# Neighbourhood attention in a transformer block on one core: transposes in 64-row pairs, division after the values, pool outputs as operands at once, first output tiles among the last units

## The chip, the cores and the metric

The kernel runs on one core of a Trainium2 chip. The metric is the device time of one execution in microseconds; three runs of the kernel before gave a median of 1085.58 us (1084.1 to 1085.93). Engines are named as in the profile: PE multiplies matrices and transposes, PEld is its weight load, ACT and DVE work elementwise (ACT: copies, exponentials, squares; DVE: sums, products, minima), POOL does small jobs, SP issues most DMAs. Matrix products accumulate in PSUM, in banks of 128 x 512 float32; everything else lies in SBUF.

## What is computed

One layer of a diffusion transformer block for 1024 latent tokens (a grid of 16 rows by 64 columns) and 256 context tokens, width 1024, all in float32:

```python
h_x = _modulate(x, g_pre_mix, sh1, sc1)              # RMSNorm, scale and shift
h_c = _modulate(ctx, g_pre_mix, csh1, csc1)
u_x, q_x, k_x, v_x = _project(h_x, w_in)             # 8 heads of 64
u_c, q_c, k_c, v_c = _project(h_c, w_in)
s_loc = where(col_mask, q_r @ k_window * scale + bias(rpb), -inf)   # 8 rows x 16 columns
s_ctx = q_r @ k_c * scale                                           # all context keys
p = softmax(concat(s_loc, s_ctx))
attn_x = p_loc @ v_window + p_ctx @ v_c
d = windowed_mean(u_x) - u_x                         # windows 2, 4, 8, 16 by channel group
mix_x = concat(d @ pool_w * pool_scale, attn_x) @ w_out
x = x + gt1 * _rmsnorm(mix_x, g_post_mix)
y_x = square(relu(_modulate(x, g_pre_mlp, sh2, sc2) @ w1)) @ w2
x = x + gt2 * _rmsnorm(y_x, g_post_mlp)
```

## The kernel before

Large products are done in a split form: each float32 operand is written as a rounded high part (a cast, on ACT) and the remainder (a subtraction, on DVE), and `three` (lines 167 to 170) adds high x high, high x low and low x high. Smaller products, among them the scores and values of the attention, are plain float32.

Stages in order of time: the inputs are normalised and transposed; `k`, `v`, `u` and `q` are projected (to about 237 us); the attention runs in units (237 to 368); the output projection `w_out` runs in two halves of 512 columns with 8 token tiles each (`out_group`, from 368); then the MLP, which uses some two thirds of the time.

**Buffers.** `act` holds 33 pages of 128 x 1024 (`page`), `wraw` 4 raw weight tiles (`load`, tag `raw`), `whl` 8 tiles of high or low weights. A new tile of a pool waits until the one whose place it takes has been read for the last time. PSUM has 8 banks: in the attention `ps_s` holds the scores (two tiles of two banks), `ps_t` transposed probabilities (3 banks), `ps_o` the output (1 bank).

**The pool mixer.** For each of 4 groups `pooled` makes the differences `dT` on DVE; `pool_out` multiplies them by `pool_w` on PE and ACT writes the scaled result back into the page `u` (`yT`). These products stand between the `u` and `q` projections, one group late. Later, in eight of the attention's steps (`SPLITS`), `pool_split` splits half a page each into the `mix` operands of the output projection. `background` carries the sums over `w_mod` for the later gates: each step is one weight load and one DVE addition into a page (`acca`, `accb`), and `mod_gate` closes a sum with matrix products (`pga`, `pgb`) on PE.

**A unit** is one pair of heads `j` and one strip of 8 grid columns `m`: 32 units, 128 queries each, all 16 rows of the strip. `scores` computes for both heads (64 rows of the array each) 384 local and 256 context scores (256 and 256 for the two edge strips), and DVE adds the bias table and takes the minimum (scores are negated). `exps` takes exponentials with their sums on ACT. `shares` multiplies the probabilities by the reciprocal sums on DVE. `turn` transposes the probabilities in blocks of 128 x 128 on PE (5 per head, 4 at the edges), `turn_kept` copies them from PSUM on ACT. `values` multiplies them with `v` into `po`, which collects four units; then ACT and DVE split it into `mix` (lines 738 and 739).

**The order** of PE, ACT, DVE and SP in the attention is as written (`in_order`, line 754). The loop's step `i` issues the scores of unit `i`, the transposes of unit `i - 2`, the exponentials of unit `i`, the division of unit `i - 1` and the values of unit `i - 3`; it has three more steps than there are units. The raw output weights are loaded in step 20 and split from step 32 on.

**The output projection**, lines 806 to 819: a tile is 24 matrix products of 512 columns (8 blocks in `order`, three each) into a bank of its own; ACT takes its mean square, and after it DVE multiplies it by the gate `G1` into `mp1`.

Of the kernel before, what the change touches and what calls it, by code (L numbers as in the profile page):

```python
# [79 lines left out]
def hybrid_block(ctx, tc, x, ctx_in, w_mod, b_mod, gp1, gp2, w_in, pool_w, rpb, w_out, w1, w2, vectors,  # L80
# [136 lines left out]
    with tc.tile_pool(name="ps1", bufs=8, space=PSUM) as ps1, tc.tile_pool(name="tmp1", bufs=3) as tmp:  # L217
# [310 lines left out]
        yT, dT = [], []  # L528

        def pooled(g):  # L530
            up, w = yT[g], WINDOWS[g]
# [30 lines left out]
        def pool_out(g, dp):  # L562
            dv = dp.rearrange("p (r m c) -> p m r c", r=QR, m=NM)
            for b in range(2):
                ps = bank(f"py{g}_{b}")
                nc.tensor.matmul(ps, pwt[:, g, :], dv[:, 4 * b : 4 * b + 4], start=True, stop=True)
                nc.scalar.activation(yT[g][:, b * 512 : (b + 1) * 512], ps, AF.Identity, scale=pscol[:, g : g + 1])

        for g in range(4):
# [6 lines left out]
            yT.append(up)  # L576
            dT.append(pooled(g))
            if g:
                pool_out(g - 1, dT[g - 1])
# [41 lines left out]

        for j in range(4):
            queries(j, 0, bank(f"pq{j}_0"), 3 if j > 1 else 0)
            if j == 2:
                pool_out(3, dT[3])
        for j in range(2):
            if j == 0:
                mask_page()
                tables(0)
            queries(j, 1, bank(f"pq{j}_1"), 5 - 5 * j)  # L630


    mix = [[None] * 8 for _ in range(2)]
    with (
        tc.tile_pool(name="ps_s", bufs=2, space=PSUM) as ps_s,
        tc.tile_pool(name="ps_t", bufs=3, space=PSUM) as ps_t,
# [7 lines left out]
        probs, least, sums, turns, turned, outs = {}, {}, {}, {}, {}, {}  # L644
# [42 lines left out]
        def shares(i):  # L687
            ri = sm(f"ri_{i}", 2, 4)
            nc.vector.reciprocal(ri, sums[i])
            for e in range(2):  # L690
                nc.vector.tensor_scalar_mul(probs[i, e], probs[i, e], ri[:, e : e + 1])  # L691

        def turn(i, e):
            j, m = units[i]
            if e < 2:
                if e == 0:
                    turns[i] = [page(f"pt{i}").rearrange("p (e i t) -> p e i t", e=2, i=4), None]
                t = bank(f"T{i}_{e}")
                for c in range(4):
                    nc.tensor.transpose(t[:, c * P : (c + 1) * P], probs[i, e][:, c * P : (c + 1) * P], ident)  # L700
                turned[e] = t
            elif 0 < m < NM - 1:
                t = bank(f"T{i}_x")
                for e in range(2):
                    nc.tensor.transpose(t[:, e * P : (e + 1) * P], probs[i, e][:, 4 * P : 5 * P], ident)
                turned[2] = t

        def turn_kept(i, e):
            if e < 2:
                nc.scalar.copy(turns[i][0][:, e], turned.pop(e).rearrange("p (i t) -> p i t", i=4))  # L710
            elif 2 in turned:
                px = page(f"px{i}")[:, : 2 * P].rearrange("p (e t) -> p e t", e=2)
                nc.scalar.copy(px, turned.pop(2)[:, : 2 * P].rearrange("p (e t) -> p e t", e=2))
                turns[i][1] = px

        def values(i):
            j, m = units[i]
            b = m // 4
            if m % 4 == 0:
                outs[j, b] = ps_o.tile([P, 512], F32, tag="po", name=f"po{j}_{b}")  # L720
            po = outs[j, b]
# [6 lines left out]
            pt, px = turns[i]  # L728
            for c, v in enumerate(vs):
                for e in range(2):  # L730
                    f = (2 * j + e) * HD
                    nc.tensor.matmul(po[e * HD : (e + 1) * HD, (m % 4) * P : (m % 4 + 1) * P], v[:, f : f + HD],  # L732
                                     pt[:, e, c] if c < 4 else px[:, e], start=(c == 0), stop=(c == len(vs) - 1))
            if m % 4 == 3:
                mp = page(f"mix{b}_{4 + j}", F32R)
                hi, lo = (mp[:, o : o + 512].rearrange("p (m t) -> p m t", t=P) for o in (0, 512))
                pv = po.rearrange("p (m t) -> p m t", t=P)[:, :, ::-1]
                nc.scalar.copy(hi, pv)
                nc.vector.tensor_tensor(lo, pv, hi.bitcast(F32), sub)
                mix[b][4 + j] = mp  # L740
# [7 lines left out]
        def pool_split(n):  # L748
            b, g = n // 4, n % 4
            mp = page(f"mix{b}_{g}", F32R)  # L750
            split(yT[g][:, b * 512 : (b + 1) * 512], mp[:, :512], mp[:, 512:])
            mix[b][g] = mp

        with in_order(ET.PE, ET.Activation, ET.DVE, ET.SP):
            for i in range(N + 3):
                if i < N and units[i][1] == 2 and units[i][0] < 3:
                    tables(units[i][0] + 1)
                if i < N:
                    scores(i)
                if 1 < i <= N + 1:  # L760
                    for e in range(3):
                        turn(i - 2, e)
                    for e in range(2):
                        turn_kept(i - 2, e)
                if i < N:
                    exps(i, 0)
                if 1 < i <= N + 1:
                    turn_kept(i - 2, 2)
                full = i > 2 and units[i - 3][1] % 4 == 3
                if i < N and not full:  # L770
                    exps(i, 1)
                if i < 2:
                    queries(2 + i, 1, bank(f"pq{2 + i}_1"), 3 if i == 0 else 99)
                if 0 < i <= N:
                    shares(i - 1)
                if i > 2:
                    values(i - 3)
                if i < N and full:
                    exps(i, 1)
                if i in SPLITS:  # L780
                    pool_split(SPLITS.index(i))
                if i == 20:
                    for kk in kks:
                        raw_o[0, kk] = load(f"wo0_{kk}", pair(w_out, kk, 0, 512))
                if i >= N:
                    wo[kks[i - N]] = high_low(f"wo0_{kks[i - N]}", raw_o[0, kks[i - N]])

    with tc.tile_pool(name="ps2", bufs=8, space=PSUM) as ps2:
# [4 lines left out]
      with ExitStack() as tmp2:  # L793
        tmp = tmp2.enter_context(tc.tile_pool(name="tmp2", bufs=4))

        wo[kks[3]] = high_low(f"wo0_{kks[3]}", raw_o[0, kks[3]])
        for kk in kks:
            raw_o[1, kk] = load(f"wo1_{kk}", pair(w_out, kk, 512, 512))
        G1 = gate_page("a")


        order = (4, 5, 6, 0, 1, 2, 3, 7)
        ssm = [sm(f"ssm{h}", NT) for h in range(2)]
        mp1 = [page(f"mp1_{t}") for t in range(NT)]

        def out_group(h):
            w = wo if h == 0 else {kk: high_low(f"wo1_{kk}", raw_o[1, kk]) for kk in kks}
            hs = slice(h * 512, (h + 1) * 512)
            for t in range(NT):
                b, i = t // 4, t % 4  # L810
                ps = bank(f"pw{h}_{t}")
                for n, k in enumerate(order):
                    mp = mix[b][k]
                    three(ps, mp[:, i * P : (i + 1) * P], mp[:, 512 + i * P : 512 + (i + 1) * P],
                          wk(w, k, 0, 0, 512), wk(w, k, 1, 0, 512), n == 0, n == 7)
                jk = tmp.tile([P, 512], F32, tag="t", name=f"jo{h}_{t}")
                mean_square(jk, ps, ssm[h][:, t : t + 1])
                nc.vector.tensor_tensor(mp1[t][:, hs], ps, G1[:, hs], mul)  # L818
                yield t

        for _ in out_group(0):
# [61 lines left out]
        for t in out_group(1):  # L883
# [411 lines left out]
```

## Time and profile before

| what | value |
|---|---|
| median of three runs | 1085.58 us |
| the profiled execution | 1083.97 us, span of its instructions 1082.2 us |
| granted PE clock, mean | 0.997 of full speed |
| attention, first scores to first output product | 237.69 to 368.66 us |
| output projection, first half | 368.66 us on, 8 tiles |
| MLP, first product | 459.35 us |

A row of the profile's groups gives line, engine, operation, tile written <- tiles read, array rows*columns, shape and count, then busy time, mean duration of one, and idle time before it with what ended it. A row of the timeline starts with the start and the length. The chain of waits is followed back from the last instruction, each piece with its start and length. A matmul's duration contains a fixed time after its columns have streamed, so matmuls that follow each other overlap in it.

### The profile page before, as it was taken

To read this page: it belongs to the slowest core of one execution; us is meant where nothing else is said; L and a number is where in the kernel's file an instruction comes from. 1 tells how busy PE (TensorE), PEld (TensorE's weight loads), DVE (VectorE), ACT (ScalarE), POOL (GpSimd) and SP (SyncE) were. 2 spreads that over 40 slices of the span, in tenths; PEclk is the share of its full clock that TensorE was granted. 3 is DMA by queue.
4 is the path that set the end of the run, shared out by engine and by line. 5 is a ranking of instruction groups with operands and counts; after the bars stand their busy time and mean duration, and the time that the engine had idled before them with its cause. 6 is when DMAs were issued, how large, how long until landed. Compare 5 with 4: busy or idle time off the path is not lost.

```text
span 1082.2 us, 14471 instructions
## 1 busy us (share of the span) xinstructions
PE 1064.0 (98%) x5505; PEld 866.8 (80%) x5505; DVE 684.8 (63%) x1036; ACT 519.3 (48%) x877; POOL 63.4 (6%) x109
## 2 busy tenths in 40 slices
PE   7999999999999999999999999999999999999997
PEld 6788887777777788887888888888888888888885
DVE  5546624555887515599986776665576657556576
ACT  6553021316888613677555545554454334334341
POOL 2020000051220001210000000000000000000001
PEclk9999999999999999999999999999999999999999
DMA  9906740250020307454764444535597775546556
GB/s 342 312 20 207 248 149 0 98 169 2 20 98 1 98 1 220 130 185 140 239 212 149 163 148 132 189 107 180 198 375 252 258 264 178 211 156 213 175 179 210
DMA packets 94265, 179.32 MB, mean 166 GB/s; under 512 B 6898, under 2 KB 39154, under 8 KB 94196
## 3 DMA queue, kind: packets, MB, share of 16 engines
q1 hardware_dynamic: 76644, 144.80, 40.5%
q10 hardware_dynamic: 16272, 29.40, 7.3%
q0 software_dynamic: 1280, 4.21, 1.1%
q8 instruction: 43, 0.70, 0.3%
q14 instruction: 26, 0.21, 0.1%
HBM read 140.62 MB, written 37.76 MB: 165 GB/s over the span
## 4 chain that ended last, share of the span: by engine, by line
PE 91%; ACT 3%; DVE 3%; issue 1%; DMA 1%; POOL 1%; SPq 0%; POOLq 0%; DVEq 0%; ACTq 0%
PE pk L374 4%; PE S L662 4%; PE po L732 3%; PE T L700 3%; PE pyv L168 3%; PE pyz L169 3%; PE pyz L168 3%; PE pyx L169 3%; PE phv L170 3%; PE phz L170 3%; PE pyv L169 3%; PE pyx L170 3%; PE phv L168 3%; PE phz L168 3%; PE phv L169 3%; PE phz L169 3%
## 5 line engine op out<-in xcount | busy, mean ns | idle before, releaser
L945 ACT ACTIVATE c<-c 128x512 f32<-128x512 f32 x48 | 30.4, 634 | 59.7 <-DVE c L1044 23.8
L676 DVE CUSTOM_DVE_ANT_0 sp<-S,tab 128x640 f32<-128x640 f32 (+1 forms) x56 | 42.8, 801 | 21.1 <-PE S L662 21.1
L685 ACT ACTIVATE sp<-sp,nm 128x640 f32<-128x640 f32 (+1 forms) x64 | 52.0, 813 | 7.0 <-DVE nm L676 6.9
L144 DVE TENSOR_TENSOR wpS<-S,wpS 128x512 fp32r<-128x512 f32 x64 | 43.8, 690 | 12.7 <-ACT wpS L143 12.7
L168 PE MATMUL phx<-thB,wpA 128*128 128x512 f32 x128 | 50.0, 391 | 0.9 <-ACT s L1003 0.9
L170 PE MATMUL phx<-thB,wpA 128*128 128x512 f32 x128 | 49.9, 390 | 0.0
L169 PE MATMUL phx<-tlB,wpA 128*128 128x512 f32 x128 | 49.8, 389 | 0.0
L143 ACT CAST wpS<-S 128x512 fp32r<-128x512 f32 x64 | 39.1, 616 | 17.7 <-PE phy L170 7.5
L710 ACT COPY pt<-T 128x512 f32<-128x512 f32 x64 | 34.4, 591 | 15.7 <-PE T L700 13.5
L139 POOL TENSOR_TENSOR ry<-vy,nhalf 128x1 f32<-128x1 f32 x8 | 4.4, 550 | 601.9 <-DVE vy L137 601.9
L700 PEld LDWEIGHTS T<-ident,sp 128*128 128x128 f32 x256 | 27.4, 141 | 10.8 <-ACT sp L685 4.6
L700 PE MATMUL T<-ident,sp 128*128 128x128 f32 x256 | 34.9, 279 | 0.4 <-DVE sp L691 0.4
L946 ACT ACTIVATE c<-c 128x512 f32<-128x512 f32 x48 | 30.4, 632 | 9.7 <-DVE sa L1016 8.9
L818 DVE TENSOR_TENSOR mp<-pw,Ga 128x512 f32<-128x512 f32 x16 | 11.0, 689 | 36.6 <-ACT jo L130 36.6
L691 DVE TENSOR_SCALAR sp<-sp,ri 128x640 f32<-128x640 f32 (+1 forms) x64 | 32.2, 545 | 1.1
L604 POOL TENSOR_TENSOR tab<-msk,U 128x128 f32<-128x128 f32 x48 | 28.1, 620 | 63.1 <-DMA U<-in_rpb 63.1
L1052 DVE TENSOR_TENSOR c<-phz,u 128x512 f32<-128x512 f32 x16 | 11.1, 692 | 32.1 <-PE phz L170 32.1
L130 ACT ACTIVATE jo<-pw 128x512 f32<-128x512 f32 x16 | 9.6, 598 | 40.9 <-PE pw L170 40.9
L168 PEld LDWEIGHTS phx<-thB,wpA 128*128 128x128 f32 x128 | 24.0, 188 | 6.2 <-ACT s L1003 1.3
L662 PE MATMUL S<-kT,q 64*128 64x384 f32 (+1 forms) x128 | 28.9, 495 | 0.0
L170 PEld LDWEIGHTS phx<-thB,wpA 128*128 128x128 f32 x128 | 24.0, 188 | 5.2 <-DVE wpA L144 0.2
L169 PEld LDWEIGHTS phx<-tlB,wpA 128*128 128x128 f32 x128 | 24.0, 188 | 5.0
(881 smaller groups left out, 3262.0 us busy)
## 6 DMA issues: line engine op xcount, KB each, us to landing
b<-in_w SPq DMA_DIRECT2D x64, 512.0 KB, 4.5
hrS<-hdS SPq DMA_DIRECT2D x32, 512.0 KB, 5.5
hrA<-hdA SPq DMA_DIRECT2D x24, 512.0 KB, 5.2
wm<-in_w_mod SPq DMA_DIRECT2D x16, 512.0 KB, 9.7
wa_0w<-in_w SPq DMA_DIRECT2D x16, 512.0 KB, 5.6
wa_1w<-in_w SPq DMA_DIRECT2D x16, 512.0 KB, 4.1
hdA<-c ACTq DMA_DIRECT2D x32, 256.0 KB, 2.1
hdS<-sa ACTq DMA_DIRECT2D x32, 256.0 KB, 4.3
```

The costliest lines, as they stand in the source:

```text
L143: nc.scalar.copy(hi, src)
L144: nc.vector.tensor_tensor(lo, src, hi.bitcast(F32), sub)
L168: nc.tensor.matmul(ps, ahi, bhi, start=first, stop=False, skip_group_check=more)
L169: nc.tensor.matmul(ps, ahi, blo, start=False, stop=False, skip_group_check=more)
L170: nc.tensor.matmul(ps, alo, bhi, start=False, stop=last, skip_group_check=more)
L374: nc.tensor.matmul(pks[b][j], wk(wgt, k, low, j * P, P), r, start=(k == 0 and n == 0), stop=(k == KT - 1 and n == 2))
L662: nc.tensor.matmul(S[e][:, c0 : c0 + keys.shape[1]], q[hs, cols], keys[hs], start=True, stop=True)
L676: nc.vector.tensor_tensor_reduce(out=to, in0=s, in1=bt, scale=1.0, scalar=BIG, op0=add, op1=ALU.min, accum_out=nm)
L685: nc.scalar.activation(sp, sp, AF.Exp, bias=least[i, e], scale=-1.0, accum_out=sums[i][:, e : e + 1])
L700: nc.tensor.transpose(t[:, c * P : (c + 1) * P], probs[i, e][:, c * P : (c + 1) * P], ident)
L710: nc.scalar.copy(turns[i][0][:, e], turned.pop(e).rearrange("p (i t) -> p i t", i=4))
L732: nc.tensor.matmul(po[e * HD : (e + 1) * HD, (m % 4) * P : (m % 4 + 1) * P], v[:, f : f + HD], pt[:, e, c] if c < 4 else px[:, e], start=( ...
```

## The change

The unit's transposes become pairs: the upper and the lower 64 query rows of a block of probabilities are transposed separately, each into a PSUM bank of its own, so that `T` has one bank per row half that holds all eight blocks of both heads. The probabilities are no longer divided. Instead `share` spreads the reciprocal sums over 64 columns per head, and one more pair of transposes turns them. This and the fifth blocks go into the free columns of the values' PSUM tile (`sides` of `pa`), and one ACT copy, `fifth_kept`, brings them to SBUF. `weighed` multiplies the values by the turned reciprocals, one step after the values. Of the two `T` banks ACT copies one and DVE the other.

`pool_out` writes the high part on ACT and the low part on DVE straight from PSUM into `mix`; half of these tiles take the four places of `wraw`. All four groups stand after the first query product of the second half. The background sums end with the queries 3 of the first half. The output weights go to pages, are loaded in steps 9, 14, 20 and 24 and split in halves in eight steps; low parts are made one step after high parts. Output tile 0 is computed in steps 32 to 34, tile 1 after them, both in the two halves of one score tile `po`; the rest follow in `out_group` as before.

```diff
-            if g:
-                pool_out(g - 1, dT[g - 1])
...
+                mp = page(f"mix1_{g}", F32R) if b else wraw.tile([P, 1024], F32R, tag="raw", name=f"mix0_{g}")
+                nc.scalar.activation(mp[:, :512], ps, AF.Identity, scale=pscol[:, g : g + 1])
+                nc.vector.scalar_tensor_tensor(mp[:, 512:], ps, pscol[:, g : g + 1], mp[:, :512].bitcast(F32), mul, sub)
...
+        for j in range(4):
+            queries(j, 0, bank(f"pq{j}_0"), (1, 2, 3, 99)[j])
+        mask_page()
+        tables(0)
+        queries(0, 1, bank("pq0_1"), 0)
+        for g in range(4):
+            pool_out(g)
+        queries(1, 1, bank("pq1_1"), 0)
...
-        tc.tile_pool(name="ps_t", bufs=3, space=PSUM) as ps_t,
+        tc.tile_pool(name="ps_t", bufs=2, space=PSUM) as ps_t,
...
+        pa = ps_o.tile([P, 1024], F32, tag="pa", name="pa")
+        sides = pa.rearrange("p (h f) -> p h f", h=2)[:, :, 256:448]
...
-            for e in range(2):
-                nc.vector.tensor_scalar_mul(probs[i, e], probs[i, e], ri[:, e : e + 1])
+            shares[i] = att.tile([P, P], F32, tag="ri", name=f"rb{i}", bufs=2)
+            nc.vector.tensor_copy(shares[i].rearrange("p (e t) -> p e t", e=2),
+                                  ri.rearrange("p (e o) -> p e o", o=1).to_broadcast([P, 2, HD]))
...
+            def both(to, src):
+                for h, hs in enumerate(halves):
+                    nc.tensor.transpose(to(h), src(hs), ident[hs, hs])
+            both(lambda h: sides[:, h, :HD], lambda hs: shares[i][hs])
+            for e in range(2 if inner else 0):
+                both(lambda h: sides[:, h, (e + 1) * HD : (e + 2) * HD], lambda hs: probs[i, e][hs, 4 * P : 5 * P])
+            for c in range(4):
                 for e in range(2):
+                    o = (4 * e + c) * HD
+                    both(lambda h: t[h][:, o : o + HD], lambda hs: probs[i, e][hs, c * P : (c + 1) * P])
+        def fifth_kept(i):
+            n = (3 if 0 < units[i][1] < NM - 1 else 1) * HD
+            fifths[i] = att.tile([P, 384], F32, tag="px", name=f"px{i}", bufs=4).rearrange("p (h t) -> p h t", h=2)
+            nc.scalar.copy(fifths[i][:, :, :n], sides[:, :, :n])
...
+        def weighed(i):
+            j, m = units[i]
+            if m % 4 == 0:
+                mixed[j, m // 4] = page(f"f{j}_{m // 4}")[:, :512]
+            to = mixed[j, m // 4].rearrange("p (m h t) -> p m h t", h=2, t=HD)[:, m % 4, ::-1, ::-1]
+            nc.vector.tensor_tensor(to, pa[:, (i % 2) * P : (i % 2 + 1) * P].rearrange("p (h t) -> p h t", h=2),
+                                    fifths[i][:, :, :HD], mul)
...
-        SPLITS = (7, 8, 15, 16, 23, 24, 31, 32)
+        LOADS, HALVES = (9, 14, 20, 24), (13, 17, 19, 21, 25, 27, 29, 30)
...
+            for i in range(N + 4):
...
+                if i > 3:
+                    weighed(i - 4)
+                low()
+                if i > 8 and i % 8 == 7:
+                    mixed_split(i // 8 - 1, 1)
+                if i > 0 and i % 8 == 0:
+                    mixed_split(i // 8 - 1, 0)
+                if i in HALVES:
+                    weight_split(HALVES.index(i))
                 if i < N:
                     scores(i)
                 if 1 < i <= N + 1:
+                    turn(i - 2)
+                    fifth_kept(i - 2)
                 if i < N:
                     exps(i, 0)
                 if 1 < i <= N + 1:
+                    turn_kept(i - 2, 0, nc.scalar.copy)
+                if i < N:
+                    exps(i, 1)
+                if 1 < i <= N + 1:
+                    turn_kept(i - 2, 1, nc.vector.tensor_copy)
...
                 if 0 < i <= N:
+                    share(i - 1)
+                if 2 < i <= N + 2:
                     values(i - 3)
+                if i == N:
+                    po = ps_s.tile([P, 1024], F32, tag="S", name="po")
                 if i >= N:
+                    out_sums(po[:, :512], wo, 0, ((0, 1), (2, 3, 4), (5, 6, 7), ())[i - N])
+            out_kept(0, 0, po[:, :512], page("jo0_0")[:, :512])
+            mixed_split(3, 1)
+            low()
+            out_sums(po[:, 512:], wo, 1, range(8))
+            out_kept(0, 1, po[:, 512:], page("jo0_1")[:, :512])
...
-        for _ in out_group(0):
+        for _ in out_group(0, range(2, NT)):
             pass
```

More of the change, by code (lines that the diff above doesn't have):

```diff
@@ L685, in exps, with share @@
             nc.scalar.activation(sp, sp, AF.Exp, bias=least[i, e], scale=-1.0, accum_out=sums[i][:, e : e + 1])
-        def shares(i):
-            ri = sm(f"ri_{i}", 2, 4)
+        def share(i):
+            ri = sm(f"ri_{i}", 2, 2)
             nc.vector.reciprocal(ri, sums[i])
-            for e in range(2):
[L691 to L703, printed above, removed]
-                for e in range(2):
-                    nc.tensor.transpose(t[:, e * P : (e + 1) * P], probs[i, e][:, 4 * P : 5 * P], ident)
-                turned[2] = t
@@ new lines, in turn @@
+        def turn(i):
+            inner = 0 < units[i][1] < NM - 1
+            t = [bank(f"T{i}_{h}") for h in range(2)]
+            turned[i] = t
+            halves = [slice(h * HD, (h + 1) * HD) for h in range(2)]
+            def both(to, src):
[5 more added lines that the diff above has]
+            for c in range(4):
+                for e in range(2):
+                    o = (4 * e + c) * HD
+                    both(lambda h: t[h][:, o : o + HD], lambda hs: probs[i, e][hs, c * P : (c + 1) * P])
@@ L731, in values @@
                     f = (2 * j + e) * HD
[L732 to L740, printed above, removed]
+                    nc.tensor.matmul(pa[e * HD : (e + 1) * HD, cols], v[:, f : f + HD],
+                                     turns[i][:, e, c] if c < 4 else fifths[i][:, :, (e + 1) * HD : (e + 2) * HD],
+                                     start=(c == 0), stop=(c == len(vs) - 1))
@@ new lines, in weight_load, with out_sums @@
+        def weight_load(h, kk):
+            raw_o[h, kk] = page(f"wor{h}_{kk}")
+            nc.sync.dma_start(raw_o[h, kk].rearrange("p (a f) -> p a f", a=2), pair(w_out, kk, h * 512, 512))
+        order = (4, 5, 6, 0, 1, 2, 3, 7)
+        ssm = [sm(f"ssm{h}", NT) for h in range(2)]
+        mp1 = {}
+        def out_sums(ps, w, t, ns):
+            b, i = t // 4, t % 4
+            for n in ns:
+                k, mp = order[n], mix[b][order[n]]
+                three(ps, mp[:, i * P : (i + 1) * P], mp[:, 512 + i * P : 512 + (i + 1) * P],
+                      wk(w, k, 0, 0, 512), wk(w, k, 1, 0, 512), n == 0, n == 7)
```

120 lines of the change are left out of this document (48 added, 72 removed).

## The prediction

> **What bounds the kernel now.** I read the page first, then the chain of waits in order of time, then single stretches.
>
> ```profile
> span 1082.2 us, 14471 instructions
> PE 1064.0 (98%) x5505; PEld 866.8 (80%) x5505; DVE 684.8 (63%) x1036; ACT 519.3 (48%) x877; POOL 63.4 (6%) x109
> ```
>
> PE is busy nearly throughout, so a gain must be PE work removed or one of its few gaps closed. The busy times of the stretches that the diff touches (the units, their tail, the first output half), columns stretch, then PE, PEld, DVE, ACT and POOL:
>
> ```profile
> 253.00:358.00 105.00, 105.00 (x1040) 79.64 (x1037) 82.88 (x216) 89.42 (x208) 12.25 (x24) 1.00 0.10 31
> 358.00:368.00 10.00, 8.55 (x106) 7.25 (x104) 7.71 (x16) 9.63 (x20) 0.00 (x0) 1.00 0.06 13
> 368.00:418.00 50.00, 49.34 (x218) 40.87 (x219) 13.15 (x16) 10.99 (x22) 0.00 (x0) 1.00 0.27 82
> ```
>
> Through the units PE has no idle time, at a granted clock of 1.00, with ACT at 85% and DVE at 79%. The chain gives the pace and the ends:
>
> ```profile
> 234.48 0.38 issue
> ...
> 236.86 0.70 DVE accb L199
> 237.69 1.14 PE S L662 x8
> ...
> 253.78 1.98 PE S L662 x7
> ...
> 357.11 1.06 PE S L662 x8
> ...
> 367.92 0.69 DVE mix L739
> 368.66 0.50 PE pw L168
> ```
>
> Unit 3 starts at 253.78 and unit 31 at 357.11: 28 steps in 103.3 us, 3.69 each. One inner step on PE (first fence) and on its weight loads (second):
>
> ```profile
> 266.23 0.60 PE L662 MATMUL S<-kcT,q 64*128 64x256 f32 x4
> 266.76 1.09 PE L700 MATMUL T<-ident,sp 128*128 128x128 f32 x8
> 267.69 0.38 PE L705 MATMUL T_x<-ident,sp 128*128 128x128 f32 x2
> ```
>
> ```profile
> 265.48 0.30 PEld L662 LDWEIGHTS S<-kT,q 64*128 64x128 f32 x4 [0.17 <-DVE sp L691]
> 266.75 0.86 PEld L700 LDWEIGHTS T<-ident,sp 128*128 128x128 f32 x8 [0.33 <-ACT sp L685]
> 268.00 0.63 PEld L732 LDWEIGHTS po<-pt,v 128*64 128x64 f32 x12 [0.17 <-issue]
> 269.24 0.30 PEld L662 LDWEIGHTS S<-kcT,q 64*128 64x128 f32 x4 [0.17 <-DVE sp L691]
> ```
>
> Scores take 265.48 to 266.75 (1.27), transposes to 268.00 (1.25), values to 269.24 (1.24): 3.76 in all.
>
> **The turn (64-row pairs).** An inner unit had 10 full transposes, an edge unit 8; now 11 and 9 pairs, each two 64-row transposes that move 64 columns, one pair of them for the reciprocal sums. The single durations:
>
> ```profile
> L662 PEld LDWEIGHTS S<-kT,q x128: 182/186/187, 238.0 to 357.6; 64*128 64x128 f32 x128
> ...
> L662 PE MATMUL S<-kT,q x128: 376/482/587, 238.2 to 357.8; 64*128 64x384 f32 x96, 64*128 64x256 f32 x32
> ```
>
> ```profile
> L700 PEld LDWEIGHTS T<-ident,sp x256: 137/141/146, 252.7 to 364.3; 128*128 128x128 f32 x128
> L700 PE MATMUL T<-ident,sp x256: 272/273/332, 252.7 to 364.4; 128*128 128x128 f32 x128
> ```
>
> A full transpose starts every 0.11 us: the two T_x lie in 0.38, and 0.38 - 0.273 = 0.11. The scores are already 64-row pairs: four 256-column matmuls of 0.376 lie in 0.60, so the last pair starts 0.60 - 0.376 = 0.22 after the first: two at once, at 0.22 per 256 columns. A 64-column pair is then 0.055. Its weights: four score loads of 0.187 lie in 0.30, so two run together and the next two start 0.11 later; a transpose's load is 0.046 shorter, which leaves 0.06 for a pair of loads. So a pair costs 0.06 if loads and matmuls overlap as in the scores, 0.11 if something keeps the old rate, and 0.22 if nothing overlaps. I take 0.06, as the scores are the nearest row: same row halves, two banks. The turn falls from 1.10 to 0.66.
>
> Between scores and transposes the loads now idle 0.33. Between one score pair and the next there is no such stretch on PE (0.22 per pair is streaming alone), and the new turn has the scores' 64x128 shape; so I count none, with 0.15 per step (4 us over 28) as the bound if it stays. The Trainium skill (TensorEngine Tiling, Key Properties) says that a change of the tiling mode drains the engine. By that rule the stretch goes, as counted; the three idle stretches of the weight loads, all at a change of shape, agree with it.
>
> **What then ends the step.** The values do not wait for the turn alone. In the changed program's own order every unit's first values matmul waits for ACT's copy of the side strip (the reciprocals and fifth blocks) of the next unit, because both lie in one tile `pa`. The rows for ACT and DVE, columns line, operation, count, busy, mean:
>
> ```profile
> L685 ACT ACTIVATE sp<-sp,nm 128x640 f32<-128x640 f32 x46 | 38.7, 842 | 0.5 <-DVE nm L676 0.5
> L710 ACT COPY pt<-T 128x512 f32<-128x512 f32 x58 | 31.2, 589 | 15.6 <-PE T L700 13.5 <-issue 1.4
> ...
> L713 ACT COPY px<-T_x 128x256 f32<-128x256 f32 x22 | 8.1, 369 | 0.0
> ```
>
> ```profile
> L676 DVE CUSTOM_DVE_ANT_0 sp<-S,tab 128x640 f32<-128x640 f32 x46 | 36.0, 821 | 15.7 <-PE S L662 15.6
> L691 DVE TENSOR_SCALAR sp<-sp,ri 128x640 f32<-128x640 f32 x46 | 23.4, 551 | 0.8
> ...
> L739 DVE TENSOR_TENSOR mix<-po,mix 128x512 fp32r<-128x512 f32 x7 | 4.8, 692 | 4.3 <-ACT mix L738 4.3
> ...
> L689 DVE RECIPROCAL ri<-su 128x2 f32<-128x2 f32 x29 | 4.6, 160 | 0.0
> ```
>
> The strip of 384 columns lies between 0.369 (256) and 0.589 (512): 0.48. From the first strip matmul: two more pairs 0.12, the last one's own time 0.22 (0.273 less 0.055), hand-over 0.04, copy 0.48, hand-over 0.06 (368.60, the end of the mix subtraction, to 368.66): 0.92. The main pairs end within 0.66 plus the 0.17 drain and hide under it. Then values 1.24 and scores up to their last streamed column, 1.19 (266.23 + 0.22 + 0.22 - 265.48): 3.35 per step against 3.69. Edge units are shorter, and steps with a weight or mix half to split are longer; I let these cancel and use 3.36: 28 x 0.33 = **9.2 us less**.
>
> Is there room? ACT: two exponentials 1.68, one T copy 0.59, strip 0.48, and 15 halves of 0.6 over 28 steps, 0.32: 3.07 of 3.36. DVE loses two multiplications (1.02) and gains a T copy (0.69, by the subtraction from PSUM), a 128-column broadcast (0.11 to 0.55; I take 0.2) and the product with the reciprocal (0.17 to 0.69; 0.25): with the bias sums 1.56, reciprocal 0.16 and halves 0.37 that is 3.23. Both fit, neither with much to spare; at the upper bounds DVE has 4.02 and would set the step (see the rivals).
>
> **The front.** All four pool groups' matmuls move from the `u` and `q` stages to behind the queries 0 of the second half; the count is unchanged, so PE time is too. The adaLN sums for the last gate must be complete sooner:
>
> ```profile
> 171.35 1.72 PE py L566 x4
> ```
>
> ```profile
> 216.48 0.95 POOL L185 MEMSET accb<- 128x1024 f32 x1 [139.24 <-ACT u L567]
> ```
>
> ```profile
> 221.16 1.28 DVE L190 SCALAR_TENSOR_TENSOR accb<-wmb_0w,sx,accb 128x1024 f32<-128x1024 f32 x1 [14.31 <-DMA accb<-in_b_mod]
> ```
>
> ```profile
> 233.42 1.34 DVE L190 SCALAR_TENSOR_TENSOR accb<-wmb_7w,sx,accb 128x1024 f32<-128x1024 f32 x1
> ```
>
> That page came free only with the last pool copy; in the changed program it waits for the last `u` copy, some 20 us sooner, and its eight loads and additions (13.6 us, 221.16 to 234.76) are needed four pool groups (6.9) and one query product (5.4) sooner, at 222. I count the 0.38 of waiting as saved; if the sums came late the price would be at most those 12 us, so I keep +3 as bound. The 0.88 before the first scores stays: now they wait for the copy of the last queries, 0.6. Writing the pool results as operands at once takes 8 casts and 8 subtractions out of the units and puts 8 subtractions into a stretch where DVE is half idle: nothing on PE's path. **0.4 less**, and 0.3 for the one turn before unit 3.
>
> The four `mix0` tiles sit in the weight buffers until the fourth tile of the second output half, so the MLP's first loads are issued some 15 us later, two of the residual loads behind them on SP's queue:
>
> ```profile
> 410.54 0.37 SPq L148 DMA_DIRECT2D wa0w<-in_w  x1
> ```
>
> ```profile
> 457.75 0.63 ACT L143 CAST wpA<-wa0w 128x512 fp32r<-128x512 f32 x1
> ```
>
> The first use is at 457.75, 9 us earlier now: some 20 us are left for four loads. On SP the output weights are spread ahead of the bias tables' loads, with whole units in between. Both cost nothing; without that cover a load of 6 to 8 us would show.
>
> **The tail.** From unit 31's start to the third output tile: before, 11.55 to the first tile and two tiles of 24 x 0.226 (49.34 / 218) = 5.43, 22.4 together, with PE's longest idle time, 1.7:
>
> ```profile
> PE pw L168 <- DVE mix L739: 1.7, 1, 1.7
> ```
>
> After: unit 31's step 3.35; last but one turn, values and 6 products 3.7; last turn, values and 9 products 4.15; last values and 9 products 3.2: 14.4, and tile 0 is done. But tile 1 accumulates in the other half of the same PSUM tile `po`, and in the changed program its first matmul waits for DVE's gated copy of tile 0; tile 2 waits likewise for tile 1's. The price of one such wait, from an output tile:
>
> ```profile
> 417.53 0.39 PE L170 MATMUL pw<-wo_3h,mix 128*128 128x512 f32 x1
> ...
> 418.01 0.60 ACT L130 ACTIVATE jo<-pw 128x512 f32<-128x512 f32 x1 [3.81 <-PE pw L170]
> ...
> 418.73 0.69 DVE L818 TENSOR_TENSOR mp<-pw,Ga 128x512 f32<-128x512 f32 x1 [3.08 <-ACT jo L130]
> ```
>
> The last matmul has streamed at 417.76, DVE ends at 419.42, and PE needs 0.06 and a load: 1.85. Then 14.4 + 1.85 + 5.43 + 1.85 = 23.5: **1.1 more**; without the waits it would be 2.6 less. Nothing else moves behind it.
>
> **Sum.** -9.2 - 0.4 - 0.3 + 1.1 = -8.8. The profiled execution took 1083.97, span 1082.2, and becomes 1075.2; the median of the runs, 1085.58, lies 1.6 higher, so I predict **1077**.
>
> **Rivals.**
> 1. The pairs do not overlap, weight loads holding 0.11 per pair. Turn 1.21, step 1.27 - 0.15 + 1.21 + 0.17 + 1.24 = 3.74 at best: no gain in the units (+1), tail +1.7, front -0.4: 1087. For it: no 64-row transpose is in the trace. Against: the score loads run two at once. Chance 0.12.
> 2. Slower: the strip copy becomes the pacer because ACT and DVE are late. Place: the values' wait on ACT. It decides once a step passes 3.69, so 0.33 late. Price: the 15 steps with a half to split hold the strip back by the whole cast, 0.6, and DVE's additions at upper bounds add 0.25 to every step: 3.36 + 0.32 + 0.25 = 3.93, 28 x 0.24 = +6.7, tail +1.1: 1093. For it: ACT's 85% now; against: the strip copy comes right behind the previous unit's last exponential, with 0.5 to 1 us of slack. Chance 0.09.
> 3. Nothing overlaps, 0.22 a pair: turn 2.42, step about 4.9, +35 us, 1120. Against it stand four score loads of 0.187 in 0.30. Chance 0.02. The Trainium skill (TensorE: Matmul & The Clock Gate, LDWEIGHTS) says that a load's time goes by its columns, not by its rows, so 64 rows would load no faster than 128 and the loads would double; no 64-row transpose load is in this trace to test it.
> 4. More gain: edge units shorten their steps (strip of 128 columns, 0.27; average 3.15) and nothing collides: -15, no waits at `po` -3.7: 1067. Chance 0.10.
>
> **How the numbers follow.** My forecast has 0.67, with 1072 to 1082 as its own range. No change is within 0.2%, 1083.4 to 1087.8. Faster: 0.67 + 0.10 + 0.02 of rival 1 = 0.79; same: 0.06 of rival 1; slower: the rest of it with rivals 2 and 3, 0.15. The range 1067 to 1087 leaves out rivals 2 and 3 and part of 4.
>
> **What would show it.** Two 64-row transposes starting together with pairs every 0.06 confirm the turn; 0.11 makes rival 1. PE idle ahead of the values, ended by ACT's strip copy, confirms the new pacer; such waits above 0.7, or PE idle ahead of the scores ended by DVE, make rival 2. Two gaps of about 1.8 must stand before output tiles 1 and 2, and none before the last gate's sums. The MLP should last as long as before; if it does not, the held weight buffers are the cause and the prediction is wrong there.

## The result, and the profile after

The changed kernel takes 1073.62 us (median of 4 runs, 1073.15 to 1073.95), the kernel before in the same comparison 1085.31: a ratio of 0.9893 with a 95% interval of 0.9876 to 0.991. The prediction was 1077, with 1072 to 1082 as the forecast's own range. Two rows of the page of after, against those of before:

```profile
span 1071.4 us, 15228 instructions
...
PE 1048.6 (98%) x5873; PEld 857.9 (80%) x5873; DVE 686.0 (64%) x1072; ACT 504.8 (47%) x849; POOL 55.6 (5%) x109
```

PE is still busy 98% of a span that is 10.8 us shorter, and it has 368 instructions more. The time between fixed points, both kernels measured on PE's starts (first scores 237.69 and 236.73, unit 3 at 253.70 and 252.66, unit 31 at 357.04 and 344.61, third output tile at 379.67 and 368.78):

| part | predicted | measured |
|---|---|---|
| up to the first scores | -0.4 | -0.96 |
| units 0 to 2 | -0.3 | -0.08 |
| unit 3 to unit 31, 28 steps | -9.2 | -11.39 |
| unit 31 to the third output tile | +1.1 | +1.53 |
| all behind it | 0 | +0.10 |
| sum | -8.8 | -10.80 |

Of the 0.96, 0.50 lie ahead of the first product `pk` (at 23.92 and 23.42; in all traces of this study it starts between 22.4 and 25.2, so this is not the change); 0.47 are left. Of the 3.4 between 1077 and 1073.62, 2.0 are in this table; the rest is mostly that the prediction started from a median 1.6 above the profiled execution of the kernel before, and that of the changed kernel lies only 0.5 above its own. That part is chance, and the 0.50 ahead of `pk` as well.

The 28 steps, as busy time in a stretch (columns: stretch, its length, PE, PEld, DVE, ACT, POOL busy, granted clock, DMA share, GB/s); first before, then after:

```profile
253.70:357.04 103.34, 103.34 (x1026) 78.42 (x1025) 81.78 (x213) 88.14 (x206) 12.25 (x24) 1.00 0.10 32
```

```profile
252.66:344.61 91.95, 89.19 (x1348) 71.72 (x1348) 81.70 (x238) 79.14 (x184) 10.47 (x24) 1.00 0.13 42
```

DVE's work is the same, ACT's is 9 us less, and PE now has 2.8 us of idle time. One inner step after, PE and then its weight loads in the timeline (`pa` takes the strip, that is reciprocals and fifth blocks, and the values):

```profile
282.03 0.92 PE L665 MATMUL S<-kT,q 64*128 64x384 f32 x4
282.78 0.60 PE L665 MATMUL S<-kcT,q 64*128 64x256 f32 x4
283.21 0.22 PE L707 MATMUL pa<-ident,rb 64*128 64x64 f32 x2
283.27 0.29 PE L707 MATMUL pa<-ident,sp 64*128 64x64 f32 x4
283.39 0.67 PE L707 MATMUL T<-ident,sp 64*128 64x64 f32 x16
284.13 0.88 PE L740 MATMUL pa<-pt,v 128*64 128x128 f32 x12
...
285.37 0.92 PE L665 MATMUL S<-kT,q 64*128 64x384 f32 x4
```

```profile
282.46 0.52 PEld L665 LDWEIGHTS S<-kcT,q 64*128 64x128 f32 x4
283.00 0.14 PEld L707 LDWEIGHTS pa<-ident,rb 64*128 64x128 f32 x2
...
284.13 0.64 PEld L740 LDWEIGHTS pa<-pt,v 128*64 128x64 f32 x12 [0.21 <-ACT px L720]
...
285.37 0.30 PEld L665 LDWEIGHTS S<-kT,q 64*128 64x128 f32 x4 [0.17 <-issue]
```

The step is 285.37 - 282.03 = 3.34. Three pairs start within 0.18 (283.21 to 283.39): 0.06 each. Between scores and turn the loads show no idle stretch; between strip start and values lie 0.92, and what ends them is ACT's strip copy. The tail:

```profile
PE pw L168 <- DVE mp L800: 1.5, 1, 1.5
PE po L168 <- DVE mp L800: 1.5, 1, 1.5
```

Both output tiles 1 and 2 wait for DVE's gated copy of the tile ahead of them.

### The profile page after: what moved, and what is told of

It reads as the page before. It is cut to its first block, busy times and chain, and to the rows that moved or that the text cites. A ratio compares the mean times of both kernels' runs of the same rounds, so it can differ in the third digit from the quotient of the medians.

```text
span 1071.4 us, 15228 instructions
## 1 busy us (share of the span) xinstructions
PE 1048.6 (98%) x5873; PEld 857.9 (80%) x5873; DVE 686.0 (64%) x1072; ACT 504.8 (47%) x849; POOL 55.6 (5%) x109
## 4 chain that ended last, share of the span: by engine, by line
PE 87%; ACT 5%; DVE 4%; issue 1%; DMA 1%; POOL 1%; SPq 0%; DVEq 0%; POOLq 0%; ACTq 0%
PE pk L374 4%; PE pyv L168 3%; PE pyz L168 3%; PE pyx L169 3%; PE pyx L168 3%; PE phz L170 3%; PE phv L170 3%; PE phv L169 3%; PE phz L169 3%; PE pyv L170 3%; PE pyz L170 3%; PE pyv L169 3%; PE pyz L169 3%; PE phv L168 3%; PE phz L168 3%; PE pyx L170 3%
## 5 line engine op out<-in xcount | busy, mean ns | idle before, releaser
L740 PE MATMUL pa<-pt,v 128*64 128x128 f32 x352 | 25.9, 279 | 2.3 <-ACT px L720 1.1
L170 PE MATMUL phv<-thT,wpS 128*128 128x512 f32 x64 | 24.9, 389 | 0.0
L168 PE MATMUL phy<-thT,wpS 128*128 128x512 f32 x64 | 24.9, 389 | 0.0
L169 PE MATMUL phy<-tlT,wpS 128*128 128x512 f32 x64 | 24.9, 389 | 0.0
L170 PE MATMUL phy<-thT,wpS 128*128 128x512 f32 x64 | 24.9, 389 | 0.0
L168 PE MATMUL phz<-thT,wpS 128*128 128x512 f32 x64 | 24.9, 389 | 0.0
```

The source lines that it names most:

```text
L168: nc.tensor.matmul(ps, ahi, bhi, start=first, stop=False, skip_group_check=more)
L169: nc.tensor.matmul(ps, ahi, blo, start=False, stop=False, skip_group_check=more)
L170: nc.tensor.matmul(ps, alo, bhi, start=False, stop=last, skip_group_check=more)
L740: nc.tensor.matmul(pa[e * HD : (e + 1) * HD, cols], v[:, f : f + HD], turns[i][:, e, c] if c < 4 else fifths[i][:, :, (e + 1) * HD : (e + ...
```

## The experiments

The kernel before took 1084.2 to 1084.4 beside these runs, about 1 less than beside the changed kernel, so medians of different runs that differ by about 1 us do not settle an order; such differences are read from the 28 steps in the traces, unit 3 to unit 31.

**1. Row halves apart.** The sixteen main transposes of a unit, first eight of the upper half, then eight of the lower.

```diff
-            for c in range(4):
-                for e in range(2):
-                    o = (4 * e + c) * HD
-                    both(...)
+            for h, hs in enumerate(halves):
+                for c in range(4):
+                    for e in range(2):
+                        o = (4 * e + c) * HD
+                        nc.tensor.transpose(t[h][:, o : o + HD], probs[i, e][hs, c * P : (c + 1) * P], ident[hs, hs])
```

> The changed kernel with the sixteen main 64-row transposes of a unit issued as eight of the upper row half and then eight of the lower one, so that no two row halves run side by side; the strip's pairs stay as they are. Theory (the pairs gain because two row halves overlap, and the values otherwise wait for the strip copy, 0.92 us after the strip's start): the main part grows from 0.50 to 16 x 0.06 = 0.96, its end passes the strip copy, the step grows by 0.35 to 0.45, 32 units: +11 us, 1085 (1082 to 1088). Rival (a 64-row transpose is simply half as long, and order does not matter): 1074. Rival (single ones run at 0.11): +0.9 a step, 1102.

Measured 1077.15 (ratio 0.9935, 0.992 to 0.995): a loss of 3.5 against the changed kernel, a third of what the theory gave. The main transposes of one unit:

```profile
285.27 0.97 PE L716 MATMUL T<-ident,sp 64*128 64x64 f32 x16
```

0.97 against 0.67 for the pairs. The last one takes 0.22 of it, so 16 start within 0.75, where one behind the other at 0.06 they would need 0.94: the second block starts while the first still runs. A step takes 3.50 instead of 3.34, since a part of the 0.30 lies under the strip copy. So two halves do run side by side, and the order matters, but less than all or nothing.

**2. Strip last.** The strip's pairs behind the main pairs.

> The changed kernel with the strip's pairs (reciprocals and fifth blocks) after the unit's main pairs in place of ahead of them; the same instructions. Theory (the values' first matmul waits for ACT's copy of the strip): that copy starts 0.50 later in each of 32 steps, the step grows by 0.5, +16 us at most, 1088 (1084 to 1091). Rival (the values wait for PE's own work or for the T copies): within 1 us of 1073.6.

Measured 1085.72 (1.0011, 1.0002 to 1.002), as the theory said: the whole gain is gone by the order of three pairs.

```profile
PE pa L740 <- ACT px L720: 14.7, 28, 0.6
```

All 28 steps wait for the strip copy, 14.7 / 28 = 0.53 each, and the steps from unit 3 to 31 take 103.43, as long as before the change.

**3. Output tiles 0 and 1 in two PSUM tiles.** `po` becomes two score tiles.

> The changed kernel with the output tiles 0 and 1 accumulated in two score tiles in place of the two halves of one. Theory (PE stands twice for 1.85 because both halves are one tile, so that tile 1's first matmul waits for DVE's product of tile 0, and tile 2's for that of tile 1): both waits go, -3.3 us, 1070.3 (1069.5 to 1071.5). Rival (the wait comes back at another place, for a bank or for the last mix split): less than 1 us, 1073.

Measured 1071.93 (0.9885, 0.987 to 0.99), half of the gain expected.

```profile
PE pw L168 <- DVE mp L800: 1.6, 1, 1.6
```

The wait ahead of tile 1 is gone, so sharing `po` was its cause. The one ahead of tile 2 stays: it is no matter of the shared tile. Tile 2 is the first of a new PSUM pool that takes the place of the attention's pools. In the program as built it lies in bank 0 and tile 1 in banks 2 and 3, and its first product still waits for DVE's copy of tile 1, the last reading of the old pools; no run takes this wait away. The 1.7 of before stood at the same place.

**4. All tiles behind the units.**

```diff
-                if i >= N:
-                    out_sums(po[:, :512], wo, 0, ((0, 1), (2, 3, 4), (5, 6, 7), ())[i - N])
...
-        for _ in out_group(0, range(2, NT)):
+        for _ in out_group(0, range(NT)):
```

> The changed kernel with all eight output tiles of the first half behind the units, as before. My theory: the early tiles gained nothing. They fill PE during the last units, but pay two waits of 1.50; without them one wait (for the last mix subtraction, 1.72 in the kernel before) and the short strip waits remain, so from the start of unit 31 to the third tile some 21.9 us pass instead of 24.16: 1071.3 (1070 to 1073). Rival: the early tiles fill gaps of the last units that now come back, and the time is that of the changed kernel or more, 1073.6 to 1076.

Measured 1071.33 (0.988, 0.9865 to 0.9894). PE's waits from unit 31 on:

```profile
PE pa L707 <- DVE f L750: 0.9, 2, 0.5
PE pa L740 <- DVE f L750: 0.6, 1, 0.6
PE pa L740 <- ACT px L720: 0.5, 2, 0.3
PE pw L168 <- DVE f L750: 0.4, 1, 0.4
```

2.4 us of short waits stand against 4.0 in the changed kernel, two of 1.5 among them, and from unit 31 to the third tile 21.8 us pass instead of 24.2: the early tiles cost some 2 us.

**5. Main pairs alone.** The kernel before with its main blocks in pairs; `T_x` stays in full transposes, the division where it was, ACT copies all.

> The kernel before with only the eight main blocks of a unit transposed in 64-row pairs into one bank per row half; the fifth blocks are transposed whole, the probabilities are divided as before, ACT makes all copies. Theory (the gain of the units is PE's transposes alone): the main part goes from 0.87 to 0.50 and the drain ahead of it, 0.15, goes; a drain comes ahead of the whole fifth blocks; step 3.69 to about 3.40, -8 us, 1077 (1075 to 1079.5). Rival (the relief of DVE and ACT by the later division is needed): ACT at 3.2 per step and DVE hold it back, less than 3 us gained.

Measured 1080.38 (0.9958, 0.9942 to 0.9975), between theory and rival.

```profile
253.60:351.13 97.53, 96.96 (x1248) 74.99 (x1248) 80.94 (x212) 86.82 (x204) 12.44 (x24) 1.00 0.11 34
```

The steps gain 5.8, and inner ones take 3.38, nearly as in the changed kernel. But the loads of the scores now wait for DVE in 17 steps, for 0.34 on average where the change of shape alone costs 0.17:

```profile
PEld S L662 <- DVE nm L676: 5.7, 17, 0.6
```

Some 2.3 of the 5.8 are given back behind the units, 1.6 of them by the granted clock of the profiled execution (last section).

**6. One pool half instead of eight** in the units, on top of run 5; the others are left out, which changes the result.

```diff
+            if n:
+                mix[b][g] = mix[0][0]
+                return
```

> The kernel before with main pairs alone (1080.4), and seven of the eight halves of the pool results not split in the units: the first half's operand stands in for them, so the first four blocks of the output projection are wrong copies of one. My theory: the pairs alone gained less than PE's own sum because DVE and ACT could not follow in the steps that carry two halves (3.5 to 3.9 us against 3.38): 1077.5 (1076.5 to 1079). Rival: the division's two multiplications on DVE are what holds the scores in every edge step, and leaving out halves brings under 1 us: 1079.5 to 1080.8.

Measured 1074.65 (0.991, 0.9895 to 0.9924), beyond the theory.

```profile
254.43:348.03 93.60, 93.24 (x1248) 74.00 (x1248) 78.65 (x207) 84.06 (x199) 12.25 (x24) 1.00 0.11 35
```

Five of the seven halves left out stood in these 28 steps (8, 15, 16, 23 and 24) and cost 3.9 there; of the rest, 1.6 are the clock, which stayed up here. With the division left on DVE, but these halves gone, the steps come within 1.7 of the changed kernel's.

**7. The halves spread**, on top of run 5.

```diff
-        SPLITS = (7, 8, 15, 16, 23, 24, 31, 32)
+        SPLITS = (4, 8, 13, 16, 21, 24, 29, 32)
```

> The kernel before with main pairs alone, and its eight halves of the pool results split in steps 4, 8, 13, 16, 21, 24, 29 and 32 instead of 7, 8, 15, 16, 23, 24, 31 and 32, so that they no longer follow the mix halves of steps 6, 14, 22 and 30 one by one. With pairs alone the steps from unit 3 to 31 took 97.5 us, with one half left of the eight 93.6, in the changed kernel, with as many halves spread, 91.9. Theory: it is the place of the halves that costs, three in a row: 95 (94 to 96) for the units and 1077.5 (1076 to 1079) in all. Rival: their number costs wherever they stand, and the units stay at 97 or more, 1079.5 to 1081.

Measured 1081.35 (0.9971, 0.996 to 0.9983): the theory falls, the steps take 98.74.

```profile
DVE mix L144 <- ACT mix L143: 9.3, 7, 1.4
```

Spreading them this way brings nothing. What this row offers instead: DVE stands 1.3 ahead of each of seven subtractions until ACT has made the cast that it needs. With the mix halves such waits come to 11.8 here, 8.0 in run 5 and 2.9 in run 6; in the changed kernel, which subtracts one step later, there is none, with 13 halves in these steps. That the later subtraction makes the difference was not tried by itself and stays open: the kernel before has 9.3 of such waits and no idle PE in its longer steps.

**8. Casts behind the strip copy** in the changed kernel: the lines of `mixed_split` and `weight_split` moved behind `fifth_kept`.

> The changed kernel with the casts of the weight and mix halves issued behind the strip copy on ACT instead of ahead of it. My theory: seven gaps of 0.30 to 0.46 ahead of the values, all ended by the strip copy in steps where a cast of 0.6 stands ahead of it, go: 1073.6 - 2.2 = 1071.4 (1070.8 to 1072.6). Rival: the casts now hold the exponentials and PE waits for the turn instead, 1073.6 to 1076.

Measured 1073.02 (0.9897, 0.9882 to 0.9912). The waits for the strip copy are gone (1.4 within the steps in the changed kernel):

```profile
PE S L665 <- DVE nm L679: 0.4, 1, 0.4
```

The steps take 90.9, 1.1 less; of the gaps in the tail one grew from 0.46 to 0.67. The gaps were real, but worth 1.1 in the steps, not 2.2; the medians differ by 0.6, less than the runs of either spread.

**9. The front alone.** The kernel before with the pool groups' products moved and the sums ended sooner.

> The kernel before with only the pool groups' products moved behind the queries and the gate sums ended sooner; results still go to the page and are split in the units. My theory: the gap of 0.38 ahead of the last gate's products goes, and 0.2 to 0.6 more ahead of the first scores, so 1085.3 - 1.0 = 1084.3 (1083.6 to 1085). Rival: the gain in the front hangs on something else of the change (the operands written at once), and this is no faster, 1085.3.

Measured 1097.56 (1.0124, 1.0107 to 1.0141): 13 us slower, against both. PE, and then the zeroing of the sums' page with the last of its additions:

```profile
221.37 0.39 PE L170 MATMUL pq<-hx,wq3l 128*128 128x512 f32 x1
233.87 3.78 PE L198 MATMUL pgb<-accb,ones 128*128 128x512 f32 x4 [12.11 <-DVE accb L190]
```

```profile
L185 POOL MEMSET accb<- x1: 960/960/960, 215.0 to 215.0; 128x1024 f32 x1
...
L190 DVE SCALAR_TENSOR_TENSOR accb<-wmb_7w,sx,accb x1: 1285/1285/1285, 232.5 to 232.5; 128x1024 f32<-128x1024 f32 x1
```

In the changed kernel the same zeroing starts sooner:

```profile
L185 POOL MEMSET accb<- x1: 954/954/954, 203.4 to 203.4; 128x1024 f32 x1
```

Here the pool results still go into the `u` pages, so none of these comes free, and POOL's zeroing of `accb` waits for a product of the first half's last query (210.7 to 216.2). DVE is then still at the differences of the last pool groups, whose `u` copies had to wait until 212.3, and begins the additions at 221.4.

**10. A tile of its own for these sums**, on top of run 9.

```diff
-            for acc in mod_sum(name, c, page, sx):
+            alloc = page if name == "a" else lambda n: tmp.tile([P, D], F32, tag="accb", name=n, bufs=1)
+            for acc in mod_sum(name, c, alloc, sx):
```

> The kernel before with the pool groups moved and the sums ended sooner, where that alone took 1097.56, and with a tile of its own for the last gate's sums instead of a page. Theory: the 12.11 of idle time ahead of the last gate's products is the wait for a page alone (the zeroing started at 215.0 there, at 203.4 in the changed kernel), and the granted clock after it is a consequence; with the page wait gone the front is as in the changed kernel: 1085.3 - 1.0 = 1084.3 (1083.5 to 1085.5). Rival: the loads of the sums or DVE are late whatever the page, and most of the 12 stays: 1092 to 1098.

Measured 1083.21 (0.9989, 0.998 to 0.9998): the page was the cause, and the front in itself is worth about 1 us (0.2 to 2.2 by the interval). `pgb` follows the queries without a gap:

```profile
222.57 0.40 PE L170 MATMUL pq<-hx,wq3l 128*128 128x512 f32 x1
222.81 1.88 PE L198 MATMUL pgb<-accb,ones 128*128 128x512 f32 x4
```

**11. Values ahead of the turn**, on top of run 12: PE's order scores, values, turn; the strip copy behind the first exponentials.

> As the kernel with tiles and casts behind, and in each step the values ahead of the turn on PE, and the strip copy behind the first exponentials on ACT: no values wait for the strip copy of the same step. Theory: in an inner step of 3.34 the wait for the strip copy shows only some 0.09 more than the change of shape costs anyway (0.26 against 0.17 on the weight loads), so at most 28 x 0.09 = 2.5 go: 1068.5 (1067.5 to 1070.3). Rival: the copies of T now end too late for the values, and the time is 1070 to 1075.

Measured 1091.52 (1.0068, 1.0051 to 1.0084): the rival. The steps take 106.2.

```profile
ACT sp L688 <- DVE nm L679: 28.4, 26, 1.8
...
PE pa L740 <- ACT sp L688: 5.3, 15, 0.6
```

ACT stands idle 28.4 ahead of the exponentials (7.4 in the changed kernel) and does the copies of `T` late. By the order in the program the values stand behind these and behind DVE's product of the unit before, which now comes last in the step; no run parts the two. The strip wait of the changed kernel is cheaper.

**12. Tiles and casts behind**, runs 4 and 8 together.

> The changed kernel with all eight tiles behind the units and the casts of the halves behind the strip copy, both edits of the two runs before. Theory: the two gains add, 1071.33 (tiles behind) less the 1.06 that the units from 3 to 31 lost with the casts behind: 1070.3 (1069.5 to 1071.3). Rival: the late casts lengthen the tail once no output tile covers it, 1071 to 1072.5.

Measured 1070.21 (0.9868, 0.9854 to 0.9883), as expected: faster than both kernels, 3.4 below the changed one in the medians and in the spans (1068.0 against 1071.4).

## Why the prediction was right, and where it was off

**The pairs: right.** 0.06 per pair was read off the score pairs; measured 0.06, at the loads' and matmuls' own times of

```profile
L707 PEld LDWEIGHTS T<-ident,sp x512: 136/139/142, 251.6 to 352.9; 64*128 64x128 f32 x171
L707 PE MATMUL T<-ident,sp x512: 221/222/225, 251.6 to 353.0; 64*128 64x64 f32 x171
```

Rivals 1 and 3 fall: the loads of the two halves run side by side, so twice the loads cost nothing, and run 1 shows what little is lost when they are not issued side by side. The Trainium skill (TensorE: Matmul & The Clock Gate, LDWEIGHTS) has a load's time go by its columns and not by its rows. On the rows the traces agree, 139 ns for 64 and 141 for 128; on the columns these durations do not, 137 for 64 columns (values) against 139 (transposes) and 186 (scores) for 128.

**No drain between scores and turn: right.** The loads run through, where 0.33 were idle before; only in four steps do they wait 0.2, for DVE's product. The Trainium skill (TensorEngine Tiling, Key Properties) would have it so, since the shape no longer changes.

**The strip copy as pacer: right**, in an inner step to the hundredth: 0.92 from the first strip matmul to the values, and run 2 gives the price of being late. Rival 2 did not come true: in four of the 28 steps PE waits for a copy that a cast holds back, 1.4 in all.

**The steps: the mis-sized term.** The prediction put "Edge units are shorter, and steps with a weight or mix half to split are longer; I let these cancel and use 3.36". The 12 steps of inner units alone take 3.34 to 3.36, as worked out (3.35). But of the 16 steps with an edge unit in their scores, turn or values ten take 2.86 to 3.13, and most of the halves lie in ACT's free time: 13 of the 15 fall into these steps, and only four lengthen one by more than 0.02, to 3.36 in steps 15 and 23, to 3.82 and 3.77 in steps 19 and 27. Step 19, ACT and then PE:

```profile
306.28 0.61 ACT L761 CAST wo_3h<-wor 128x512 fp32r<-128x512 f32 x1
306.79 0.47 ACT L720 COPY px<-pa 128x384 f32<-128x384 f32 x1
```

```profile
307.32 0.66 PE L740 MATMUL pa<-pt,vc 128*64 128x128 f32 x8 [0.41 <-ACT px L720]
```

The average is 91.95 / 28 = 3.28, and 28 x 0.08 = 2.2 is what was missing. Here rival 4 was half right: the edge steps are shorter, but its average of 3.15 was not reached and the waits at `po` stayed.

**Room on ACT and DVE: right**, operation for operation:

```profile
L725 DVE COPY pt<-T 128x512 f32<-128x512 f32 x29 | 19.9, 686 | 0.0
L750 DVE TENSOR_TENSOR f<-pa,px 128x128 f32<-128x128 f32 x27 | 7.7, 284 | 0.4
L694 DVE COPY rb<-ri 128x128 f32<-128x128 f32 x29 | 6.7, 229 | 1.0
```

0.69, 0.25 and 0.2 were assumed. Busy in a step were 2.92 on DVE and 2.83 on ACT, less than the 3.23 and 3.07 that were summed up. Runs 5 to 7 show that this room was needed: with pairs alone the scores wait for DVE.

**The front: right, with less to spare than was thought.** 0.47 came against 0.4. Of the 0.3 for the one turn ahead of unit 3 only 0.08 came, because its scores wait 0.36 for DVE. The prediction put the zeroing of the last gate's page behind the last `u` copy, some 20 us sooner; it came behind ACT's first query copy, at 203.4 instead of 216.5, 13 us sooner. The last addition ends at 221.34 and PE takes the sums at 221.84: that they were in time was in part luck. The bound "at most those 12 us" for sums that come late was met in run 9 by the idle time, 12.11, when the page did not come free; the whole loss was 13.3, because the clock fell as well. What the prediction did not say outright is that the two edits are one: the sums may end sooner only because the results no longer live in the `u` pages.

**The tail: right in kind, sizes off.** Both waits stand where they were put; from the last streamed column to PE's next start they take 1.66 (1.50 of it idle in the profile) instead of 1.85. Of the second, not `po` but the new pool was the cause (run 3). The 14.4 up to the last streamed column of tile 0 is 15.24, by three waits of 0.30, 0.46 and 0.20 for the strip copy and the product of the last units that were counted as covered; tile 1 takes 5.59 instead of 5.43, and the stretch before was 22.6, not 22.4. Run 4 shows that without early tiles the tail is shorter; the prediction had only weighed the waits.

**Nothing behind: right.** From the third tile on both kernels differ by 0.1.

## What to carry to other kernels

Read the rate of a new instruction form from the nearest form that already runs in it, and then ask which copy must come first: the order of three pairs here was worth as much as the whole change (run 2). Count steps by kind instead of letting short and long ones cancel. An edit that needs a buffer sooner depends on the edit that frees it; test such edits together and apart before giving either a price of its own.

## What the runs showed of the hardware

The granted clock fell after idle time, and not always alike. After the 12.11 of run 9 (columns as above, the clock is the third figure from the end):

```profile
221.70:233.90 12.20, 0.09 (x2) 0.04 (x1) 10.35 (x19) 0.00 (x0) 0.00 (x0) 0.63 0.62 215
233.90:245.00 11.10, 11.10 (x21) 4.93 (x22) 1.38 (x2) 5.15 (x8) 0.31 (x1) 0.79 0.15 42
```

The four gate products took 3.78 there and 1.88 in run 10. In run 5 the usual idle 1.71 ahead of the first output tile was enough, while the kernel before, with 1.7 at the same place, kept its clock. The traces show more than the length of the gap. In each of them the granted clock changes only at times that are whole multiples of 3.41 us apart, from 1.00 to 0.50 or back. On that grid, first run 5, then run 7, then the kernel before:

```profile
359.74:363.15 3.41, 1.62 (x22) 1.18 (x19) 2.72 (x4) 3.16 (x5) 0.00 (x0) 1.00 0.49 152
363.15:366.56 3.41, 3.41 (x10) 2.64 (x9) 1.90 (x2) 0.45 (x1) 0.00 (x0) 0.50 1.02 352
```

```profile
361.19:364.60 3.41, 1.54 (x26) 1.06 (x20) 2.72 (x3) 3.16 (x5) 0.00 (x0) 1.00 0.30 90
364.60:368.01 3.41, 3.14 (x7) 2.48 (x8) 2.53 (x3) 1.08 (x2) 0.00 (x0) 0.50 0.99 356
```

```profile
365.47:368.88 3.41, 1.69 (x25) 1.45 (x22) 2.72 (x4) 3.18 (x5) 0.00 (x0) 1.00 0.41 133
368.88:372.29 3.41, 3.41 (x16) 2.80 (x16) 2.02 (x2) 0.58 (x1) 0.00 (x0) 1.00 0.82 201
```

Where PE was busy for 1.62 and 1.54 of a window, the next one ran at half clock; after 1.69 it did not. This order holds for every window between 30 and 1060 us in all 14 traces: beside these two falls only run 9 has one, after a window with 0.35. In the first 20 us the clock also fell after windows with up to 1.8, so busy time is not the whole measure, and no run moved the limit on purpose. One such window is the 1.6 us of run 5, and run 7's trace has the same; how busy a window is depends also on where its edges fall, so this loss of runs 5 and 7 need not come back in every execution. The Trainium skill (TensorE: Matmul & The Clock Gate, Part 1: The HAM clock gate) says that an idle window of about 3.4 us throttles the clock, in windows that run freely. The length of the windows and run 9 agree with it; that a window need not be idle, but can be busy for nearly half, is what runs 5 and 7 show, and there the measurement decides.
